# Output projection with three pairs of PSUM banks: logits transposes in the tile's own banks, work ranked by tile number

## The chip, the cores and the metric

The kernel runs on one core of one Trainium2 chip. The metric is the device time of one execution in microseconds (us), median of several runs. The engines are TensorE (PE, with its weight loads as PEld), VectorE (DVE), ScalarE (ACT), GpSimd (POOL) and SyncE (SP), which here only issues transfers. PSUM, the memory that TensorE writes, has eight banks; a tile of 128 rows by 512 columns of 32-bit numbers fills one.

## The reference, cut to what matters

Two layers of a transformer with a mixture of experts (MoE). The change touches what stands in each layer between attention and MoE:

```python
o = jnp.concatenate([o_a, o_b, o_c], axis=-1) @ w_out[l]      # (1024, 1024) @ (1024, 1024)
x = layer_norm(DEEPNORM_ALPHA * x + g1 * o, ln1_g[l], ln1_b[l])
h2 = modulate(x, sh2, sc2)                                    # a second layer norm, scale and shift
# ec_moe(h2, ...): router logits h2 @ w_router, softmax over 16 experts,
# each expert takes its top 128 tokens, gated FFN, scatter-add
x = layer_norm(DEEPNORM_ALPHA * x + g2 * ec_moe(h2, ...), ln2_g[l], ln2_b[l])
```

There are 1024 latent tokens (8 tiles of 128) in both layers; in layer 0 alone the 256 context tokens (2 tiles) go the same way with weights of their own modulation. No expert can start before all 1024 tokens have their routing scores, because top-k runs over tokens.

## The kernel before, in words

One function, `p4`, holds the stage; it runs once per layer. A tile `i` goes through these steps:

- Loads on SP's queue: `ot` (the attention output, transposed, L1684, for the first two tiles its last quarter apart, L1687), `rb` (softmax denominators, L1692, two transfers), `x` (the residual, L1698; two buffers).
- Preparation: `den` (L1705) multiplies by the denominators, `ohi` (L1715 on DVE, L1717 on ACT) and `olo` (L1720) split the 32-bit operand into two parts that TensorE multiplies at full rate. From the third tile on this is POOL and ACT.
- Projection on PE: 48 matmuls of 512 columns (L1737, L1738, L1739), in 8 groups of 6, into a pair of PSUM banks `po`, one bank for each half of the 1024 columns. There are two such pairs.
- Norms in place in the pair, on DVE: gate (L1745), add the residual (L1851), statistics (L1772 twice, L1778, L1779, and a power on POOL, L1782), normalize (L1795, L1798). ACT reads the pair once for the copy `ac` that the MoE accumulates into (L1860). Then a second norm: statistics again, L1795, and two halves of L1804 that write the result to SBUF as `t`.
- Routing: 8 transposes of `t` on PE (L1882) into the banks `tp` (two, one for each half), a copy of each half to SBUF `hT` on ACT (L1887, one buffer), 8 logits products (L1896), maximum (L1900), exponential (L1904), reciprocal (L1907), scaling (L1910), one transpose of the shares (L1919) and a copy into `aff` (L1923).

Context tiles differ: ACT copies the projection out of PSUM (L1750) and POOL and DVE do the norms in SBUF. After the eighth latent tile, 16 rounds of top-8 on DVE (L2008, L2009, L2011) pick the tokens; rounds 13 to 16 of layer 0 also serve the context tiles. Then the indices drive a gather, and the MoE begins.

The order of instructions on every engine is written by a planner, `Plan`. Each operation has an engine, a planned cost, a lag until others may use its result, a list of what it needs, and slots (how many buffers of a kind exist). The planner repeatedly takes the operation that can start earliest by its own clock; among those that can start at the same time it takes the largest sum of `way` (planned time from this operation to the end of everything that depends on it) and `rank`. The two lines that decide are:

```python
first = min(t for t, o in at) + self.SLACK
t, o = min(((t, o) for t, o in at if t <= first), key=lambda c: (-c[1]["way"] - c[1]["rank"], c[0], c[1]["n"]))
```

Most operations of tile `i` have the rank `old`, which is -3 times `i` before. The engines then execute that order, in order; where real times differ from planned ones an engine stands at its next instruction.

Of the kernel before, what the change touches and what calls it, by code (L numbers as in the profile page):

```python
# [8 lines left out]
F32 = mybir.dt.float32  # L9
# [4 lines left out]
AF = mybir.ActivationFunctionType  # L14
# [195 lines left out]
class Kern:  # L210
# [1368 lines left out]
    def p4(self, l):  # L1579
        nc, d = self.nc, self.d  # L1580
# [28 lines left out]
        if not last:  # L1609
            nc.gpsimd.memset(aff[64:80], -1.0)  # L1610
        ve, ac, po, pe, sy = "dve", "act", "pool", "pe", "sync"
        P = Plan(ported=True, ot=3, rb=3, x=2, oh=3, t1=4, po=2, tp=2, hT=1, lg=2, ac=1, raw=4, w=4)
        eng = {ve: nc.vector, po: nc.gpsimd}
        tt = {ve: 1.16, po: 2.32}
        load = lambda cost, f, **k: P.op(sy, cost, f, lag=2.2, **k)
# [51 lines left out]
        for i, (t, cond) in enumerate(tiles):  # L1667
            q = {}
# [6 lines left out]
            row0 = t * 128 - ctx * NL  # L1675
            src = self.s_o[part][:, :, cs].rearrange("c p q -> p c q")
            gain, scale, shift = range(3)
            old = -3.0 * i
            H = {k: P.new(k) for k in ("ot", "rb", "x", "oh", "t1", "hT", "ac")}

            def ld_o(q=q, src=src, i=i):
# [17 lines left out]
            a = load(1.2, ld_o, new=[H["ot"]], rank=old)  # L1699
            c = load(0.4, ld_c, use=[H["ot"]], after=[a], rank=old - 20.0) if i < 2 else a  # L1700
            b = load(1.2, ld_r, new=[H["rb"]], after=late[part], rank=old)
            x = load(1.46, ld_x, new=[H["x"]], rank=old)

            def den(q=q, i=i):
                (nc.vector if i < 2 else nc.gpsimd).tensor_tensor(q["ot"][:, 0:6], q["ot"][:, 0:6], q["rb"], op=ALU.mult)  # L1705
# [22 lines left out]
            for n in range(2):  # L1728
                o = None
                for k in range(4):  # L1730
                    def mm(q=q, n=n, k=k):
                        if n == 0 and k == 0:
                            q["o"] = self.rot(ps, [128, 2, 512], F32, "po", 2)
                        o, ns = q["o"][:, n], slice(n * 512, n * 512 + 512)
                        for j in (2 * k, 2 * k + 1):
                            wh, wl = whi[k][:, j % 2, ns], wlo[k][:, j % 2, ns]
                            nc.tensor.matmul(o, q["hi"][:, j], wh, start=j == 0, stop=False)  # L1737
                            nc.tensor.matmul(o, q["hi"][:, j], wl, start=False, stop=False)  # L1738
                            nc.tensor.matmul(o, q["lo"][:, j], wh, start=False, stop=j == 7)  # L1739
                    o = P.op(pe, 1.395, mm, [parts[k], W[k], o or first], new=[hp] if n == 0 and k == 0 else [],  # L1740
                             use=[H["oh"], hw[k]] + ([hp] if n or k else []), rank=old)
                    first = first or o

                def gate(q=q, n=n, cond=cond):
                    nc.vector.tensor_tensor(q["o"][:, n], q["o"][:, n], rows[cond][0][:, n * 512:n * 512 + 512], op=ALU.mult)  # L1745

                def out(q=q, n=n):
                    if n == 0:
                        q["t1"] = self.rot(p, [128, D], F32, "t1", 4)
                    nc.scalar.activation(q["t1"][:, n * 512:n * 512 + 512], q["o"][:, n], AF.Copy)  # L1750

                def gate_c(q=q, n=n, cond=cond):
                    ns = slice(n * 512, n * 512 + 512)
                    nc.gpsimd.tensor_tensor(q["t1"][:, ns], q["t1"][:, ns], rows[cond][0][:, ns], op=ALU.mult)
                if ctx:
                    o = P.op(ac, 0.6, out, [o, *gated[-1:]], new=[H["t1"]] if n == 0 else [],
                             use=[hp] + ([H["t1"]] if n else []), rank=old)
                    gated.append(P.op(po, 1.24, gate_c, [o, lrow[cond][0], *gated[-1:]], use=[H["t1"], hrow[cond][0]], rank=old))
                else:
                    gated.append(P.op(ve, 0.68, gate, [o, lrow[cond][0], *gated[-1:]], use=[hp, hrow[cond][0]], rank=old))  # L1760
# [29 lines left out]
            def affine_o(dep, g, b, uses, new=None, q=q):  # L1790
# [16 lines left out]
                if new is None:  # L1807
                    o = P.op(ve, 1.28, f2, [o], **u)
                    return [o, o]
                o1 = P.op(ve, 0.7, lambda: f3(0), [o], new=[new], **u)  # L1810
                return [o1, P.op(ve, 0.7, lambda: f3(1), [o1], use=u["use"] + [new], rank=old)]

            def affine(dep, kind, g, b, uses, q=q):

# [58 lines left out]
            P.op(sy, 1.46, put2, o, use=[H["t1"]], lag=2.2, rank=old)  # L1873
            c = []
            for h in range(2):
                ht = P.new("tp")

                def tr(q=q, h=h):
                    tp = q["tp", h] = self.rot(ps, [128, 4, 128], F32, "tp", 2)
                    for k in range(4):  # L1880
                        kk = h * 4 + k
                        nc.tensor.transpose(tp[:, k], q["t1"][:, kk * 128:kk * 128 + 128], self.ident)  # L1882

                def cp(q=q, h=h):
                    if h == 0:
                        q["hT"] = self.rot(p, [128, KC, 128], F32, "hT", 1)
                    nc.scalar.activation(q["hT"][:, h * 4:h * 4 + 4], q["tp", h], AF.Copy)  # L1887
                z = P.op(pe, self.CT if ctx else 0.44, tr, [o[h]], new=[ht], use=[H["t1"]], rank=old)
                c.append(P.op(ac, 0.49, cp, [z, *c[-1:]], new=[H["hT"]] if h == 0 else [],
                              use=[ht] + ([H["hT"]] if h else []), rank=old))  # L1890
            hl = P.new("lg")

            def logits(q=q):
# [17 lines left out]
            o = P.op(pe, self.CG if ctx else 1.75, logits, [*c, lw], new=[hl], use=[H["hT"]], rank=old)  # L1911
            o = P.op(ve, 0.1, top, [o], use=[hl], rank=old)
            o = P.op(ac, 0.3, ex, [o], use=[hl], rank=old)
            o = P.op(ac, 0.25, share, [P.op(ve, 0.15, rel, [o], rank=old)], rank=old)
            ha = P.new("lg")

            def turn(q=q):
# [72 lines left out]
    CT, CG = 0.44, 1.75  # L1990
    KINDS = "dd", "ff"
    TE = "pp"
    LP = 0
    ER = -100.0, -100.0
    WR, WS, HD, AB = (5.0, 10.0), (8.0, 4.0), (1, 1), (5.0, 5.0)

# [528 lines left out]
```

## Time and profile before

| | |
|---|---|
| median of 3 runs | 3002.39 us (2997.36 to 3002.39) |
| the profiled execution's own time | 2998.05 us |
| its span, first to last instruction | 2996.3 us |
| TensorE's mean granted clock | 0.936 of full |
| busy share of the span: PE, DVE, ACT, POOL | 88%, 73%, 53%, 30% |
| layer 0: first projection matmul to first top-k instruction | 601.6 to 780.4 us |
| layer 1: the same | 2148.4 to 2321.4 us |

The shares over the whole span are averages over stages with different limits; the two stretches in the last lines are where the change acts.

### The profile page before, as it was taken

The page shows a single profiled execution, that of the slowest core. Times are in us where ns is not written, and L with a number is a line of the kernel's source. Part 1 is how long each engine was busy: PE and PEld are TensorE (multiplying, and loading weights), DVE is VectorE, ACT ScalarE, POOL GpSimd, SP SyncE. Part 2 cuts the span into 40 slices and gives each one's busy share as a digit, 9 for nine tenths or more (in the row PEclk, how much of TensorE's full clock was granted, in tenths as well). Part 3 has the DMA queues.
Part 4 walks back from the last instruction along what each step waited for, and adds up shares of the span by engine and source line. Part 5 has one row for each costly group of instructions (what it writes and reads, how often), then busy time and mean ns, then how long its engine had stood idle before and what let it go on. Part 6 is the DMA issues. An engine that isn't in the chain of part 4 may idle for free.

```text
span 2996.3 us, 37302 instructions
## 1 busy us (share of the span) xinstructions
PE 2632.8 (88%) x13657; PEld 2066.0 (69%) x13657; DVE 2186.5 (73%) x3048; ACT 1588.1 (53%) x2023; POOL 886.2 (30%) x652
## 2 busy tenths in 40 slices
PE   7998888868569999999999499999867499999995
PEld 4986444446468888888888388655556377777774
DVE  6367597456769998888887835566556788888888
ACT  4224767612245656656666353686412367777774
POOL 2045787232312120201110416685120211111113
PEclk8999999978779999999999699999977699999998
DMA  6254734472268888888886414563452699999983
GB/s 241 79 177 145 207 127 121 121 222 102 89 238 317 319 313 312 311 312 313 313 310 229 159 64 150 174 188 94 137 168 106 261 360 374 375 374 367 367 348 133
DMA packets 204352, 682.85 MB, mean 228 GB/s; under 512 B 25637, under 2 KB 97630, under 8 KB 148870
## 3 DMA queue, kind: packets, MB, share of 16 engines
q1 hardware_dynamic: 191834, 641.23, 59.2%
q0 software_dynamic: 12336, 39.25, 5.2%
q8 instruction: 107, 1.75, 0.2%
q14 instruction: 75, 0.61, 0.1%
HBM read 600.45 MB, written 79.84 MB: 227 GB/s over the span
## 4 chain that ended last, share of the span: by engine, by line
PE 58%; DVE 7%; DMA 3%; issue 2%; ACT 1%; POOL 1%; SPq 0%; DVEq 0%; POOLq 0%; ACTq 0%
PE gu L2145 12%; PE gu L2146 6%; PE gu L2184 4%; PE gu L2185 4%; PE gu L2186 4%; PE O L1183 3%; PE gu L2226 2%; PE gu L2217 2%; PE gu L2240 2%; PE gu L2227 2%; PE gu L2228 2%; PE gu L2241 2%; PE gu L2239 2%; PE pj L736 1%; PE pj L737 1%
## 5 line engine op out<-in xcount | busy, mean ns | idle before, releaser
L2071 DVE TENSOR_TENSOR lo<-raw,hi 128x2048 fp32r<-128x2048 f32 x284 | 640.7, 2282 | 6.8 <-ACT hi L2065 6.8
L2065 ACT ACTIVATE hi<-raw 128x2048 fp32r<-128x2048 f32 x289 | 551.8, 1912 | 87.2 <-PE gu L2185 39.9
L2145 PE MATMUL gu<-xt,hi 128*128 128x320 f32 x2048 | 529.6, 333 | 0.9 <-DVE xt L2131 0.9
L2146 PE MATMUL gu<-xt,lo 128*128 128x192 f32 x2048 | 513.6, 251 | 0.0
L1257 POOL TENSOR_TENSOR cy<-cy,csq 128x512 f32<-128x512 f32 (+1 forms) x300 | 386.7, 1303 | 110.4 <-ACT csq L1253 101.1
L2261 POOL DMA_INDIRECT s_acc<-yo,i x31 | 76.3, 2463 | 1121.5 <-DVE yo L2259 1121.5
L2146 PEld LDWEIGHTS gu<-xt,lo 128*128 128x128 f32 x2048 | 393.0, 192 | 0.6
L2145 PEld LDWEIGHTS gu<-xt,hi 128*128 128x128 f32 x2048 | 386.2, 189 | 1.8 <-DVE xt L2131 1.1
L1183 PE MATMUL O<-P,v 128*65 128x512 f32 (+7 forms) x592 | 280.2, 562 | 11.9 <-ACT P L1176 11.6
L1253 ACT ACTIVATE csq<-ch,cw 128x512 f32<-128x512 f32 (+1 forms) x300 | 198.9, 673 | 47.0 <-POOL cy L1257 43.6
L2184 PE MATMUL gu<-hi,xt 128*128 128x512 f32 x512 | 204.3, 399 | 0.0
L2185 PE MATMUL gu<-hi,xt 128*128 128x512 f32 x512 | 202.8, 396 | 0.0
L2186 PE MATMUL gu<-lo,xt 128*128 128x512 f32 x512 | 202.6, 396 | 0.0
L735 PE MATMUL pj<-hhi,whi 128*128 128x512 f32 (+1 forms) x512 | 188.5, 368 | 9.4 <-ACT whi L249 9.4
L737 PE MATMUL pj<-hhi,wlo 128*128 128x512 f32 (+1 forms) x512 | 188.1, 367 | 1.5 <-DVE wlo L252 1.5
L736 PE MATMUL pj<-hlo,whi 128*128 128x512 f32 (+1 forms) x512 | 188.1, 367 | 0.0
L2071 DVE TENSOR_TENSOR lo<-more,hi 128x2048 fp32r<-128x2048 f32 x80 | 182.0, 2282 | 0.0
L2065 ACT ACTIVATE hi<-more 128x2048 fp32r<-128x2048 f32 x80 | 152.1, 1906 | 19.5 <-issue 10.0
L366 DVE CUSTOM_DVE_ANT_0 adj<-adw,srow,bmod 128x1024 bf16<-128x1024 f32 x96 | 133.8, 1394 | 34.4 <-DMA adw<-in_wmt 32.7
L1176 ACT ACTIVATE P<-ST 128x512 f32<-128x512 f32 (+1 forms) x200 | 114.6, 581 | 51.7 <-PE ST L1159 28.5
L1737 PE MATMUL po<-hi,ohi 128*128 128x512 f32 x288 | 122.8, 426 | 20.3 <-DVE ohi L1715 16.9
L1739 PE MATMUL po<-hi,olo 128*128 128x512 f32 x288 | 119.2, 414 | 3.4 <-DVE olo L1720 2.6
(319 smaller groups left out, 5787.4 us busy)
## 6 DMA issues: line engine op xcount, KB each, us to landing
raw<-in_wmoe SPq DMA_DIRECT2D x289, 1024.0 KB
more<-in_wmoe SPq DMA_DIRECT2D x80, 1024.0 KB
adw<-in_wmt SPq DMA_DIRECT2D x24, 1024.0 KB
srow<-in_wmoe SPq DMA_DIRECT2D x15, 1024.0 KB
wraw<-in_win SPq DMA_DIRECT2D x26, 512.0 KB
x<-in_x SPq DMA_DIRECT2D x16, 512.0 KB
adw<-in_wmt SPq DMA_DIRECT2D x16, 512.0 KB
q<-s_q SPq DMA_DIRECT2D x64, 128.0 KB
```

The source lines that it names most:

```text
L736: nc.tensor.matmul(o[:, :w], whi[:, k], hlo[:, k, sl], start=False, stop=False)
L737: nc.tensor.matmul(o[:, :w], wlo[:, k], hhi[:, k, sl], start=False, stop=k == 7)
L1183: nc.tensor.matmul(o[:V1, o0:o0 + w], self.v[:, t["kt"], t["v"] * V1:t["v"] * V1 + V1], t["P"][:, :w], start=t["first"], stop=t["last"] is ...
L1253: nc.scalar.activation(z[:, :w], h, AF.Copy, scale=c)
L1257: nc.gpsimd.tensor_tensor(st["y"], st["y"], st.pop(("z", t))[:, :w], op=ALU.add)
L2065: self.nc.scalar.activation(h, self.S["raw", i], AF.Copy)
L2071: eng.tensor_tensor(lo, r, h.bitcast(F32), op=ALU.subtract)
L2145: nc.tensor.matmul(o[:, f, :320], hi[:, k, fs], xt[:, k], start=k == 0, stop=False)
L2146: nc.tensor.matmul(o[:, f, :192], lo[:, k, fs], xt[:, k, :192], start=False, stop=k == 7)
L2184: nc.tensor.matmul(o, xt[:, kk, 0], hi[:, k], start=kk == 0, stop=False)
L2185: nc.tensor.matmul(o, xt[:, kk, 1], hi[:, k], start=False, stop=False)
L2186: nc.tensor.matmul(o, xt[:, kk, 0], lo[:, k], start=False, stop=kk == 7)
```

## The change

It does these things in `p4`, for both layers:

- The slots `tp` (two banks) are gone and `po` has three pairs instead of two; 2x2 + 2 + 2 banks become 3x2 + 2.
- The 8 transposes of a tile write into the tile's own pair, half by half, once the second norm has read that half; ACT copies from there. The pair is held until that copy.
- Ranks go down by 12 for each tile instead of 3 (`ORD`). The residual of the second tile is raised by 5 (`XE`).
- The two halves of the last norm step no longer depend on one another, have a planned cost of 0.72 instead of 0.7, the second half a rank lower by 0.5, and both a planned lag of 1.0 (all tiles but the last). The scaling of the shares gets a planned lag of 2.0 (all tiles but the last). Lags are numbers for the planner; they put no wait into the program.
- `LP`, used nowhere, is removed.

```diff
-        P = Plan(ported=True, ot=3, rb=3, x=2, oh=3, t1=4, po=2, tp=2, hT=1, lg=2, ac=1, raw=4, w=4)
+        P = Plan(ported=True, ot=3, rb=3, x=2, oh=3, t1=4, po=3, hT=1, lg=2, ac=1, raw=4, w=4)
...
-            old = -3.0 * i
+            old = -self.ORD[l] * i
...
-            x = load(1.46, ld_x, new=[H["x"]], rank=old)
+            x = load(1.46, ld_x, new=[H["x"]], rank=old + (self.XE if i == 1 else 0.0))
...
-                            q["o"] = self.rot(ps, [128, 2, 512], F32, "po", 2)
+                            q["o"] = self.rot(ps, [128, 2, 512], F32, "po", 3)
...
-                o1 = P.op(ve, 0.7, lambda: f3(0), [o], new=[new], **u)
-                return [o1, P.op(ve, 0.7, lambda: f3(1), [o1], use=u["use"] + [new], rank=old)]
+                wait = 1.0 if i < len(tiles) - 1 else None
+                o1 = P.op(ve, 0.72, lambda: f3(0), [o], new=[new], lag=wait, **u)
+                return [o1, P.op(ve, 0.72, lambda: f3(1), [o], use=u["use"] + [new], rank=old - 0.5, lag=wait)]
...
-                ht = P.new("tp")
-
                 def tr(q=q, h=h):
-                    tp = q["tp", h] = self.rot(ps, [128, 4, 128], F32, "tp", 2)
                     for k in range(4):
                         kk = h * 4 + k
-                        nc.tensor.transpose(tp[:, k], q["t1"][:, kk * 128:kk * 128 + 128], self.ident)
+                        nc.tensor.transpose(q["o"][:, h, k * 128:k * 128 + 128], q["t1"][:, kk * 128:kk * 128 + 128], self.ident)
...
-                    nc.scalar.activation(q["hT"][:, h * 4:h * 4 + 4], q["tp", h], AF.Copy)
-                z = P.op(pe, self.CT if ctx else 0.44, tr, [o[h]], new=[ht], use=[H["t1"]], rank=old)
+                    nc.scalar.activation(q["hT"][:, h * 4:h * 4 + 4], q["o"][:, h].rearrange("p (a b) -> p a b", a=4), AF.Copy)
+                z = P.op(pe, self.CT if ctx else 0.44, tr, [o[h]], use=[H["t1"], hp], rank=old)
                 c.append(P.op(ac, 0.49, cp, [z, *c[-1:]], new=[H["hT"]] if h == 0 else [],
-                              use=[ht] + ([H["hT"]] if h else []), rank=old))
+                              use=[hp] + ([H["hT"]] if h else []), rank=old))
...
-            o = P.op(ac, 0.25, share, [P.op(ve, 0.15, rel, [o], rank=old)], rank=old)
+            o = P.op(ac, 0.25, share, [P.op(ve, 0.15, rel, [o], rank=old)], rank=old,
+                     lag=2.0 if i < len(tiles) - 1 else None)
...
-    LP = 0
+    ORD = 12.0, 12.0
+    XE = 5.0
```

## Rows read from the trace of the kernel before

**Rows 1.** The page's second part: busy tenths of PE in 40 slices of 74.9 us each.

```profile
PE   7998888868569999999999499999867499999995
```

**Rows 2.** Busy time by stretch: from:to, length, then busy us and instruction count of PE, PEld, DVE, ACT and POOL, the granted clock, the share of the DMA engines, GB/s. The first two are the stage in each layer, the third a stretch without waits at full clock, then one two-tile run of matmuls, the first halt of PE in layer 0, and the top-k of layer 0.

```profile
601.60:780.40 178.80, 135.49 (x627) 109.16 (x628) 104.36 (x170) 35.70 (x71) 43.15 (x33) 0.84 0.50 153
2148.40:2321.40 173.00, 129.82 (x584) 105.13 (x584) 105.11 (x170) 31.85 (x68) 35.12 (x28) 0.81 0.49 157
613.00:621.00 8.00, 8.00 (x36) 6.41 (x36) 3.26 (x2) 0.00 (x0) 0.00 (x0) 1.00 1.06 361
...
2271.50:2296.10 24.60, 24.48 (x100) 19.44 (x99) 9.77 (x15) 2.13 (x5) 0.54 (x1) 0.93 0.11 43
629.00:653.80 24.80, 1.11 (x5) 0.71 (x4) 15.75 (x26) 3.88 (x5) 14.31 (x10) 0.59 0.81 202
780.40:845.00 64.60, 22.48 (x108) 17.98 (x106) 57.00 (x122) 18.48 (x25) 28.61 (x17) 0.66 0.40 159
```

**Rows 3.** Waits of PE in the stage: who waited, for whom, us in total, times, the longest. The first line is layer 0, the other two layer 1.

```profile
PE tp L1882 <- DVE t L1804: 25.6, 2, 22.9
...
PE lg L1919 <- ACT e L1910: 21.7, 4, 9.1
PE tp L1882 <- DVE t L1804: 15.5, 1, 15.5
```

**Rows 4.** Groups by line in layer 1's stage (8 tiles): what one tile costs DVE. Instructions, busy us, mean ns, then idle time before them and who ended it.

```profile
L1772 DVE BATCH_NORM_STATS2 p4st<-po 128x6 f32<-128x512 f32 x32 | 21.7, 692 | 7.5 <-PE po L1739 5.3 <-ACT ac L1860 1.6
...
L1804 DVE SCALAR_TENSOR_TENSOR t<-po,p4nr,raw 128x512 f32<-128x512 f32 x16 | 11.6, 743 | 0.4 <-POOL p4nr L1782 0.3
...
L1745 DVE TENSOR_TENSOR po<-po,raw 128x512 f32<-128x512 f32 x16 | 11.2, 699 | 45.2 <-PE po L1739 44.9
L1851 DVE SCALAR_TENSOR_TENSOR po<-x,po 128x512 f32<-128x512 f32 x16 | 11.1, 696 | 0.6
L1798 DVE SCALAR_TENSOR_TENSOR po<-po,p4nr,lnb 128x1024 f32<-128x1024 f32 x8 | 10.3, 1285 | 0.3
L1795 DVE SCALAR_TENSOR_TENSOR po<-po,mv,raw 128x1024 f32<-128x1024 f32 x8 | 10.3, 1284 | 1.9 <-ACT ac L1860 1.9
L1795 DVE SCALAR_TENSOR_TENSOR po<-po,mv,lng 128x1024 f32<-128x1024 f32 x8 | 10.2, 1278 | 0.0
...
L1778 DVE BATCH_NORM_AGGREGATE mv<-p4st 128x2 f32<-128x12 f32 x16 | 3.2, 202 | 0.2
...
L1779 DVE TENSOR_SCALAR p4nr<-mv 128x1 f32<-128x1 f32 x16 | 2.5, 154 | 0.6
...
L1900 DVE TENSOR_REDUCE sm<-lg 128x1 f32<-128x16 f32 x8 | 1.3, 166 | 6.4 <-PE lg L1896 6.4
L1907 DVE RECIPROCAL sm<-sm 128x1 f32<-128x1 f32 x8 | 1.3, 157 | 1.5 <-ACT e L1904 1.5
```

**Rows 5.** The same view, layer 1, the other engines' steps of a tile.

```profile
L1887 ACT ACTIVATE hT<-tp 128x512 f32<-128x512 f32 x16 | 9.2, 595 | 10.0 <-PE tp L1882 5.5 <-PE lg L1896 4.4
L1782 POOL TENSOR_TENSOR p4nr<-p4nr,mhalf 128x1 f32<-128x1 f32 x16 | 8.7, 546 | 62.0 <-DVE p4nr L1779 61.9
...
L1860 ACT ACTIVATE ac<-po 128x1024 f32<-128x1024 f32 x8 | 8.2, 1024 | 58.7 <-DVE po L1798 49.4 <-DMA s_acc<-ac 9.3
```

**Rows 6.** Timeline of PE, single stretches: start, length, instruction, [idle before, releaser]. Two projection matmuls at full clock that are 30 matmuls apart, four transposes, the logits products of one tile (two instructions for each of 8), and the transposes of shares that end two halts, one period apart. The line at 623.14 is where the late quarter of `ot` arrived.

```profile
613.06 0.39 PE L1737 MATMUL po<-hi,ohi 128*128 128x512 f32 x1
...
620.06 0.39 PE L1737 MATMUL po<-hi,ohi 128*128 128x512 f32 x1
...
623.14 0.50 PE L1737 MATMUL po<-hi,ohi 128*128 128x512 f32 x1 [1.52 <-DVE ohi L1715]
...
680.38 0.63 PE L1882 MATMUL tp<-ident,t 128*128 128x128 f32 x4
681.28 1.96 PE L1896 MATMUL lg<-wr,hT 128*128 128x16 f32 x16 [0.27 <-ACT hT L1887]
...
2232.27 0.38 PE L1919 MATMUL lg<-ident,e 128*16 128x128 f32 x1 [9.08 <-ACT e L1910]
...
2269.65 0.38 PE L1919 MATMUL lg<-ident,e 128*16 128x128 f32 x1 [5.66 <-ACT e L1910]
```

**Rows 7.** Timelines of DVE and POOL around the first tiles of layer 0 (626 to 647) and of layer 1 (2170 to 2182): the first gate in each layer, the second tile in PSUM waiting for its residual, statistics waiting for ACT's reading of the pair, POOL at the first tile's power, and in layer 1 the gate that follows the last of the first 96 matmuls.

```profile
626.24 0.70 DVE L1745 TENSOR_TENSOR po<-po,raw 128x512 f32<-128x512 f32 x1 [2.21 <-PE po L1739]
...
639.69 0.69 DVE L1851 SCALAR_TENSOR_TENSOR po<-x,po 128x512 f32<-128x512 f32 x1 [7.32 <-DMA x<-in_x]
...
646.98 0.70 DVE L1772 BATCH_NORM_STATS2 p4st<-po 128x6 f32<-128x512 f32 x1 [1.09 <-ACT ac L1860]
...
638.03 0.57 POOL L1782 TENSOR_TENSOR p4nr<-p4nr,mhalf 128x1 f32<-128x1 f32 x1
...
2170.16 0.70 DVE L1745 TENSOR_TENSOR po<-po,raw 128x512 f32<-128x512 f32 x1 [4.09 <-PE po L1739]
...
2177.13 0.70 DVE L1745 TENSOR_TENSOR po<-po,raw 128x512 f32<-128x512 f32 x1 [2.18 <-PE po L1739]
...
2181.74 0.58 POOL L1782 TENSOR_TENSOR p4nr<-p4nr,mhalf 128x1 f32<-128x1 f32 x1
```

**Rows 8.** Timeline of DVE at the top-k: layer 0's first instruction, and its wait for the context tiles.

```profile
780.38 0.69 DVE L2008 MAX8 tv<-aff 48x8 f32<-48x512 f32 x1 [5.67 <-ACT aff L1923]
...
832.32 0.69 DVE L2008 MAX8 tv<-aff 80x8 f32<-80x512 f32 x1 [2.46 <-ACT aff L1923]
```

## The prediction

> **What bounds the kernel now.** I read the page's busy tenths first [rows 1]. Most slices have PE at 8 or 9; in the tenths 4 to 7 about slices 9 to 12 and 29 to 32 the reader sees the stages between attention and MoE, where PE stands. The change acts in two of them, so next comes busy time by stretch [rows 2]. From the first projection matmul to the first top-k instruction layer 0 takes 178.8 us with PE busy for 135.5, layer 1 takes 173.0 with 129.8: some 43 us a layer without PE. DVE is busy for 104 and 105. So no engine is full: a chain is. Whose chain, the waits of PE say [rows 3]. Layer 0 loses 25.6 us to transposes that wait for the last norm step, 22.9 of them at once, and layer 1 15.5 at once and 21.7 in four waits for the shares. PE projects two tiles, finds no free pair, and stands until DVE has carried the first of the two through both norms. The same shows from DVE's side: the gate waits 44.9 us in all for the projection [rows 4]. The engines take turns.
>
> Does the time of this stage come through to the end? Top-k needs every token, the experts need top-k, and top-k starts behind the last latent tile's copy into `aff` [rows 8]. I count a microsecond here as one of the total.
>
> **Third pair: the steady pace.** PE's work for a tile: 48 matmuls at 7.00/30 = 0.233 us [rows 6] are 11.2; 8 transposes are two groups of 0.6, logits products 1.9, the shares' transpose 0.3 [rows 6]. Sum 14.6 us. DVE's: the eleven groups add up to 94.7 us for 8 tiles, 11.8 each [rows 4]. If one tile is finished before the next is begun, DVE also stands while ACT reads the pair for `ac`: 1.09 us in the row [rows 7], so 13.0 with handovers. A pair is held for 14.6 us of PE's time and then for DVE's chain, transposes and copies, about 13 + 3: 31 us, and three pairs allow a tile each 10. So PE sets 14.6 us a tile, if it never waits. Before, two tiles take 37.4 (the halts that end at 2232.3 and 2269.7 mark the period [rows 6]), 18.7 each: 24.6 of matmuls [rows 2], then the rest of DVE's chain uncovered. I take 15.5, since DVE is at 13.0 of 14.6 and each engine runs in a fixed order.
>
> Here the page "PSUM — Partial Sum Buffer" of the Trainium skill (PSUM bank collisions raise a hardware error) speaks against the change: no two engines may touch one bank at once, two reads included. The row with 1.09 us agrees. By that rule transposes and copies also serialize inside the tile's own banks, which the old separate banks spared; since PE writes a half while ACT copies the other, the sum is the same, and if each copy of 0.6 us held up PE twice a tile it would be 1.2 us a tile more.
>
> **Third pair: the start.** Layer 0's first two tiles leave PE at 629.0, where its first halt begins [rows 2]. A third tile follows at once, its inputs having been prepared before: 11.2 us, to 640.2. The residual of the third tile can only be fetched when the first has been added (two buffers); it ended DVE's wait at 639.69 [rows 7], in time. The fourth tile needs the first pair. POOL delivered the first tile's power at 638.03 + 0.57, behind splits of later tiles [rows 7]. If that stays: 638.6, L1798 1.3, ACT's reading 1.0 with one statistics under it, the other 0.7, mean and sum 0.36, L1795 1.3, L1804 1.5 [rows 4, 5], transposes 1.2, copies 1.2 and handovers: 648. If tile rank brings the power forward nothing is lost: 640.2. I take 645. In layer 1 the same walk from 2177.1, where the first 96 matmuls end [rows 7], gives 2188.3 for the third tile, and from the power at 2181.74 [rows 7] 2191 for the fourth. I take 2191.
>
> **The tail.** After the eighth tile's last matmul: gate, addition, statistics 2.1, mean and sum 0.35, L1795 and L1798 2.6, `ac` and one statistics 1.7, mean and sum 0.35, L1795 1.3, L1804 1.4 [rows 4, 5], transposes and copy 1.2, logits 1.9, softmax 1.1, transpose and copy 0.6. That is 14.6 us, and with some twenty handovers of 0.1 us 16.5. The powers on POOL (0.55) pass beside L1795.
>
> **The sum.** From the fourth tile's start: five tiles' matmuls 56.0, the other PE work of seven tiles 7 x 3.4 = 23.8, allowance 5 x 0.9 = 4.5, tail 16.5: 100.8 us. Layer 0: 645 + 100.8 = 745.8, against 780.4: 34.6 saved. Layer 1: 2191 + 100.8 = 2291.8, against 2321.4: 29.6. Together 64 us. The profiled execution took 2998.05; the median shown is 4.3 above it. So 2934 becomes 2938.
>
> **The rest of the diff.** Rank 12 is what makes DVE finish a tile before it begins another: by the planned costs the way from a tile's last matmul to its transposes is 12.0 (gate, addition, two statistics, mean, power, two normalizations, two statistics, mean, power, normalization, last step with lag 1.0), so a gate one tile later ranks about even with the older tile's last steps and below its other ones. A matmul has 13.5 to 24 more way than its tile's transposes: those of the next tile still go before the older tile's transposes, those two tiles on mostly behind. That order is the forecast. The lags only leave room in it; price nothing, covered by the matmuls between. The first tiles' late quarter of `ot` (rank 20 lower) now passes the third tile's loads on SP's queue; between nothing and the 1.5 us that PE waited for it [rows 6]; I take nothing. `XE` moves one 0.5 MB load by a place or two: nothing, for the second tile's residual was there first. Context tiles hold their pairs until their copies; nobody comes after them. Their chain must keep up with a top-k that starts earlier: top-k waited 2.46 us for it once [rows 8]. PE is free of latent matmuls sooner, so between 0 and 5 us more saved; I take nothing. The split last step saves no work.
>
> **Rivals.**
> - *DVE becomes the bound.* Finishing tile by tile leaves it nothing to do while ACT reads (1.09), POOL raises to the power (0.55 twice, with handovers 1.4) and PE ends a half. 11.8 + 1.1 + 1.4 + 1.5 is 16 us a tile. From the first gates, 626 and 2170 [rows 7], 8 x 16 + 7 for routing gives 761 and 2305: 19 and 16 saved, 2998 - 35 + 4 = 2967. For it: the row of 1.09 and POOL's late power. Against: powers run under L1795, and next tiles' gates fill holes. Chance 0.22.
> - *One layer alone gains.* Layer 0's loads (0.81 of the DMA engines in the first halt [rows 2]) keep the fourth tile back, or the context chain sets top-k's end as the 2.46 hints: 3002 - 30 = 2972, chance 0.05.
> - *Nothing changes.* A load paces the stage, as the residual did for 7.32 us [rows 7]. But DMA falls to 0.11 in the later tiles [rows 2]. 3002, chance 0.05.
> - *Slower.* Place: PE's queue. The planner sets a tile's transposes between matmuls two tiles on; if DVE is later than planned, PE stands there with ready matmuls behind it, as it stood 9.08 us for shares [rows 6]. Price: the delay, at 14 places (7 a layer). It decides from 64/14 = 4.6 us a place; with 9 at each, 2938 + 126 = 3064. Against: the chain after the last matmul measures 9.8 to the end of L1804 without handovers, under the planned 12.0. Chance 0.08.
>
> **How the numbers follow.** Forecast 0.60, and the four rivals as given. Its own range: no stall at either start (4.8 + 2.7), pace 14.6 (9), context waits gone (5) give 2917; pace 16.5 in both layers (10) and 1.2 us for the banks over 16 tiles (19) give 2967. For 8 in 10 the range is 2915 to 2985: it takes in the two rivals that gain less and leaves no change and slower out, 0.13, with some of the edges. The three runs differ by 0.17%, so 0.2%, 6 us, is about what can be told apart. Faster 0.86, same 0.06, slower 0.08.
>
> **What would show it.** PE's waits on L1804 of 22.9 and 15.5 us fall to under 8 each, those on the shares (21.7) vanish from the middle of the stage. Its matmuls run in series longer than 96, and the granted clock of the two stretches rises above 0.84 and 0.81. DVE's gates wait some 15 us for the projection instead of 45. The first top-k instruction comes near 746, and 143 us after layer 1's first matmul (173 before). If DVE is busy 95% of the stage, the first rival holds; if transposes wait over 4 us at most tiles, the last. MoE stretches should keep their lengths; if they don't, the prediction is wrong there, not here.

## The result, and the profile after

Measured in turn on one chip, the changed kernel took 2927.44 us and the kernel before 2999.88 (medians of four runs each); the ratio is 0.9769, 95% interval 0.9738 to 0.98. Measured once more, beside two of the experiments below, it gave 2928.69 against 2996.05, ratio 0.9779 (0.9765 to 0.9792). The profiled execution took 2927.74 us; its span, 2926.0, is 70.3 less than before. One of the five executions of an experiment below (own banks and third pair) took 6457.73 us, and no profile shown is of it.

First PE's busy tenths by fortieths of the span, from the page of the changed kernel:

```profile
PE   7998888979489999999999499999996699999995
```

A slice is 73 us. Of the hollow that [rows 1] has in each layer, slice 11 is left in layer 0, the top-k behind the stage, and slices 31 and 32 in layer 1, the tail and top-k. Busy time by stretch, in the columns of [rows 2]; first the two stages (first projection matmul to first top-k instruction), then the pipelined part of each stage, and the tail of layer 1:

```profile
603.20:749.20 146.00, 138.36 (x665) 113.00 (x666) 105.01 (x175) 38.22 (x74) 49.27 (x37) 0.95 0.63 192
2112.60:2251.60 139.00, 121.21 (x584) 98.56 (x584) 105.74 (x170) 32.63 (x68) 34.05 (x28) 0.91 0.58 194
...
650.20:740.00 89.80, 88.15 (x450) 72.26 (x450) 72.42 (x124) 27.14 (x56) 24.49 (x23) 0.98 0.42 145
2157.00:2230.00 73.00, 71.54 (x367) 58.82 (x366) 61.34 (x102) 18.64 (x42) 17.30 (x18) 0.98 0.39 146
2230.00:2251.50 21.50, 9.13 (x51) 7.73 (x50) 11.94 (x21) 5.29 (x13) 1.08 (x2) 0.61 0.47 176
```

The stages went from 178.8 and 173.0 us [rows 2] to 146.0 and 138.9. Layer 1 has the same work in it, 584 instructions on PE in both, and DVE's busy time is 105 us as before; layer 0's stage has 665 on PE instead of 627, since more of the context tiles' matmuls now fall before the top-k. In the middle of either stage PE is busy for 98% at a granted clock of 0.98. The waits of PE in the two stages (for whom, us in total, times, the longest), layer 0 first:

```profile
PE po L1880 <- DVE t L1804: 4.7, 3, 3.6
PE lg L1894 <- ACT hT L1885: 0.7, 1, 0.7
...
PE po L1880 <- DVE t L1804: 9.4, 3, 7.6
...
PE lg L1918 <- ACT e L1908: 3.1, 2, 1.8
```

The 25.6 and 15.5 us on the last norm step [rows 3] are 4.7 and 9.4, and 7.6 of the 9.4 are the tail, where nothing else is left to do; the 21.7 on the shares are 3.1. DVE's gates in layer 1 wait 3.0 us for the projection, where they waited 44.9 [rows 4] and the prediction named some 15. The 70.3 us by place: layer 0's first matmul comes 1.6 us later, its stage is 32.8 shorter, the way from the first top-k instruction to the first transposes of the MoE (L2129) 3.3 shorter; layer 1's first matmul comes 35.8 earlier, so between the layers another 1.2 are gone, layer 1's stage is 34.1 shorter, and 0.4 falls behind it.

### The profile page after: what moved, and what is told of

Read it like the earlier page. It is cut to its first block, busy times and chain, and to the rows that moved or that the text cites. A ratio compares the mean times of both kernels' runs of the same rounds, so it can differ in the third digit from the quotient of the medians.

```text
span 2926.0 us, 37297 instructions
## 1 busy us (share of the span) xinstructions
PE 2619.4 (90%) x13657; PEld 2057.6 (70%) x13657; DVE 2184.7 (75%) x3048; ACT 1587.8 (54%) x2023; POOL 884.3 (30%) x652
## 5 line engine op out<-in xcount | busy, mean ns | idle before, releaser
L1737 PE MATMUL po<-hi,ohi 128*128 128x512 f32 x288 | 121.7, 423 | 21.4 <-DVE ohi L1715 18.9
L2153 ACT ACTIVATE t<-gu 128x320 f32<-128x320 f32 x128 | 55.5, 433 | 119.3 <-PE gu L2146 119.1
```

## The experiments

The change has three parts that can be had one by one: the rank of a tile (3 or 12), the place of the transposes (banks of their own kind, called separate here, or the tile's own), and the number of pairs. Three pairs with separate banks don't fit, so there are six combinations; the lags and `XE` come on top. All kernels with own banks also have the last norm step in two independent halves, as the change has; what that split does by itself was not tried. **Theory A**, the prediction's: PE stood because it found no free pair, and the third pair ends that. **Theory B**: the rank does it, because two tiles that DVE carries side by side come free together, whatever their number.

Medians in us, with the ratio to the kernel before as it was measured beside each:

| | rank 3 | rank 12 |
|---|---|---|
| two pairs, separate banks | 2998.59 (before) | with `XE` 2932.51, 0.9782 (0.9757 to 0.9806); with lags and `XE` 2933.03, 0.9793 (0.9777 to 0.9808) |
| two pairs, own banks | 2982.91, 0.9947 (0.9928 to 0.9967) | 2964.6, 0.9892 (0.9877 to 0.9907), with lags and `XE` |
| three pairs, own banks | 2963.25, 0.9879 (0.9861 to 0.9898) | 2928.69, 0.9779 (0.9765 to 0.9792), the change; without lags and `XE` 2935.52, 0.9791 (0.9774 to 0.9809) |

And the stages, from the first row of L1737 to the first of the top-k in each trace, with the period of a tile in the middle of layer 0, from the starts of its transposes (with rank 3 from the starts of blocks of matmuls):

| kernel | layer 0, us | layer 1, us | us a tile |
|---|---|---|---|
| before | 178.8 | 173.0 | 17.9 |
| rank alone (with `XE`) | 146.9 | 145.7 | 14.1 |
| rank alone with lags and `XE` | 155.3 | 142.3 | 14.0 |
| own banks alone | 171.1 | 173.1 | 16.2 |
| own banks and third pair | 166.0 | 156.0 | in blocks |
| the change with two pairs | 164.2 | 160.0 | 16.2 |
| the change | 146.0 | 138.9 | 13.0 |
| the change, second profile | 147.7 | 138.8 | 13.7 |
| the change without lags | 146.3 | 151.5 | 14.1 |
| less matmul work | 149.7 | 140.1 | 13.8 |
| less DVE work | 149.0 | 145.4 | 13.2 |
| `ac` in halves | 146.4 | 141.9 | 13.0 |
| rank 30 | 148.3 | 152.0 | 13.3 |

The two profiles of the change differ by 1.8 us in layer 0 and by 0.7 us a tile, so less than that tells nothing. The profile of the rank alone with lags and `XE` is of an execution of 2943.67 us, 10.6 above its median; in its layer 0 one wait for `ohi` at the start takes 7.8 us, where the rank alone has 2.6.

**Rank alone** (with `XE`), in the kernel before:

```
-            old = -3.0 * i
+            old = -12.0 * i
-            x = load(1.46, ld_x, new=[H["x"]], rank=old)
+            x = load(1.46, ld_x, new=[H["x"]], rank=old + (5.0 if i == 1 else 0.0))
```

> The kernel before (two pairs, separate banks for the transposes) with rank 12 a tile alone. Theory A (the pairs do it): with two pairs PE can project one tile while DVE carries the other; a pair is then held for 11.2 us of matmuls and a chain of 11 to 12 us, so a tile each 12 at the least but in strict turns with the other PE work, 16 to 18.7 us a tile: stages of 160 to 178 us, total 2965 to 3000 us. Theory B (the rank does it, the third pair adds little): stages within 4 us of 146.0 and 138.9, total 2927 to 2940 us.

It took 2932.51 us: 66 of the change's 67 to 72, with two pairs and the separate banks. Theory A falls. Its PE row in the middle of layer 0 (busy time by stretch), and then DVE in order of time (start, us, line, what; in brackets the wait before):

```profile
655.00:740.00 85.00, 84.62 (x445) 69.99 (x444) 69.35 (x115) 26.43 (x52) 23.04 (x20) 1.00 0.39 135
...
669.31 0.70 DVE L1745 TENSOR_TENSOR po<-po,raw 128x512 f32<-128x512 f32 x1 [0.46 <-PE po L1739]
...
674.10 1.28 DVE L1795 SCALAR_TENSOR_TENSOR po<-po,mv,lng 128x1024 f32<-128x1024 f32 x1
...
675.50 1.29 DVE L1798 SCALAR_TENSOR_TENSOR po<-po,p4nr,lnb 128x1024 f32<-128x1024 f32 x1
...
679.67 1.28 DVE L1795 SCALAR_TENSOR_TENSOR po<-po,mv,raw 128x1024 f32<-128x1024 f32 x1
681.06 1.41 DVE L1804 SCALAR_TENSOR_TENSOR t<-po,p4nr,raw 128x512 f32<-128x512 f32 x2
683.28 0.70 DVE L1745 TENSOR_TENSOR po<-po,raw 128x512 f32<-128x512 f32 x1 [0.81 <-PE po L1739]
```

One tile's first norm, second norm and last step stand in a row, and then comes the next tile's gate: 13.2 us from its own gate to the end of its last step. PE is busy for 84.62 of 85 us at clock 1.00: two pairs saturate it. In the kernel before DVE does this, in the same view:

```profile
666.80 0.70 DVE L1745 TENSOR_TENSOR po<-po,raw 128x512 f32<-128x512 f32 x1 [7.77 <-PE po L1739]
...
682.71 1.28 DVE L1795 SCALAR_TENSOR_TENSOR po<-po,mv,raw 128x1024 f32<-128x1024 f32 x1
683.90 1.28 DVE L1795 SCALAR_TENSOR_TENSOR po<-po,mv,lng 128x1024 f32<-128x1024 f32 x1
685.09 0.74 DVE L1804 SCALAR_TENSOR_TENSOR t<-po,p4nr,raw 128x512 f32<-128x512 f32 x1
685.75 1.28 DVE L1798 SCALAR_TENSOR_TENSOR po<-po,p4nr,lnb 128x1024 f32<-128x1024 f32 x1
686.94 0.74 DVE L1804 SCALAR_TENSOR_TENSOR t<-po,p4nr,raw 128x512 f32<-128x512 f32 x1
...
692.41 1.41 DVE L1804 SCALAR_TENSOR_TENSOR t<-po,p4nr,raw 128x512 f32<-128x512 f32 x2
```

Two tiles alternate instruction by instruction, the older one's second norm (`raw`) with the younger one's first (`lng`, `lnb`). The older one takes 20.9 us from gate to last step (666.8 to 687.7). Both pairs stay occupied meanwhile, and then both come free, at 687.7 and 693.8, within the 11.2 us of one tile's matmuls.

**Own banks alone** (two pairs, rank 3, no lags, no `XE`): the changed kernel with

```
-        P = Plan(... t1=4, po=3, hT=1, ...)
+        P = Plan(... t1=4, po=2, hT=1, ...)
-                            q["o"] = self.rot(ps, [128, 2, 512], F32, "po", 3)
+                            q["o"] = self.rot(ps, [128, 2, 512], F32, "po", 2)
-    ORD = 12.0, 12.0
-    XE = 5.0
+    ORD = 3.0, 3.0
+    XE = 0.0
...
-                wait = 1.0 if i < len(tiles) - 1 else None
+                wait = None
...
-                     lag=2.0 if i < len(tiles) - 1 else None)
+                     lag=None)
```

> Two pairs, transposes in the tile's own banks, old rank, no lags and no XE: the banks' cost alone. The pair is held longer by the second norm, transposes and copies, some 8 us a tile, and two tiles go together, so the halts of PE grow by about 8 us for each pair of tiles: with three halts that are followed by more matmuls in a layer, 20 to 24 us a layer later, total 3035 to 3050 us. If instead the shared bank costs nothing because the pair was free only at the end of both norms anyhow, the total stays at 2995 to 3005 us.

Both expectations were wrong: it gained 16 us. PE in order of time in layer 0:

```profile
650.97 1.09 PE L1880 MATMUL po<-ident,t 128*128 128x128 f32 x4 [23.30 <-DVE t L1804]
...
669.91 1.07 PE L1880 MATMUL po<-ident,t 128*128 128x128 f32 x8
672.20 0.60 PE L1737 MATMUL po<-hi,ohi 128*128 128x512 f32 x1 [1.23 <-ACT hT L1885]
```

The first halt stays (23.3 us, as the 22.9 of [rows 3]). But a pair now comes free only with the copy of its own transposes, and those follow each other on PE, so the pairs come free one after the other and the blocks of 96 matmuls break into blocks of 48: 16.2 us a tile instead of 17.9, although PE waits 0.7 to 1.2 us for ACT's copy seven times. The longer hold was priced, the regular order that it enforces was not. How much of the 16 us the split of the last norm step has in it is open.

**Own banks and third pair** (rank 3, no lags, no `XE`): as above with `po=3` and `"po", 3`.

> The third pair and the tiles' own banks, with rank 3 a tile as before, and without the lags and XE. Theory A (the pairs do it: PE stood because it found no free pair): PE goes on over the third tile as in the changed kernel, stages of 145 to 152 us in layer 0 and 138 to 145 in layer 1 against 146.0 and 138.9, total 2927 to 2942 us. Theory B (the rank does it: with rank 3 DVE still carries two tiles through the norms side by side, so that pairs come free together): PE runs three tiles and then stands for 10 us or more, some 16 to 17 us a tile, stages near 160 and 153, total 2955 to 2970 us.

It took 2963.25 us, half of the gain; own banks alone had 16 of these 35 us. The profile is from a second run, 2960.97 us:

> The third pair and the own banks with rank 3, once more, for an undisturbed profile (the one of the first run was taken with every matmul at twice its time). By the time of the first run, 2963.25 us median, about half of the gain is there. Theory B (the rank decides): the order of PE's queue still has two or three tiles' matmuls in one block and then a halt on the last norm step; stages of about 160 and 158 us. Theory A (the pairs decide and something small is missing): matmuls and transposes alternate tile by tile, with short waits, and what is lost sits in the tail.

```profile
639.40 0.40 PE L1739 MATMUL po<-hi,olo 128*128 128x512 f32 x1
653.72 1.09 PE L1880 MATMUL po<-ident,t 128*128 128x128 f32 x4 [13.93 <-DVE mv L1778]
656.28 1.12 PE L1880 MATMUL po<-ident,t 128*128 128x128 f32 x4 [1.47 <-DVE t L1804]
658.97 0.80 PE L1737 MATMUL po<-hi,ohi 128*128 128x512 f32 x1 [1.57 <-ACT hT L1885]
```

Three tiles' matmuls in one block, and then the halt: 19.2 us from 639.8 to 659.0 with 2.2 of transposes in it, where [rows 2] has 24.8 behind two tiles. The third pair puts the halt off by a tile; it doesn't end it. Theory B, in time and in order.

**The change with two pairs** (`po=2` and `"po", 2` alone), and **the change without own banks and third pair** (the kernel before with rank, lags and `XE`), beside **the change itself**:

> The changed kernel with two pairs instead of three, all else as in the change: transposes in the tile's own banks, rank 12, lags, XE. A pair is then held for the 11.2 us of matmuls, DVE's chain of 11 to 12 and the transposes and copies, 2 to 3: some 25 us, and two pairs give one tile each 12.5 at best; PE has to do logits and shares of older tiles in the gaps. If the third pair is what lets the rank work with the own banks: 15 to 16 us a tile instead of 14, 8 to 16 us a layer, total 2943 to 2960 us. If two pairs are enough here too: total 2925 to 2937 us.

> The kernel before with rank 12, the lags and XE: all of the change without the third pair and without the own banks. The rank alone gave 2932.51 us median. If what is left to the changed kernel, about 5 us, is owed to the lags (which cost the rank alone 7.6 us of waiting in layer 1's fourth tile): total within 4 us of the changed kernel's, 2924 to 2932 us. If it is owed to the third pair (PE projects the third tile while DVE has the first, and is never idle from 632.9 to 639.7 us): total 2930 to 2936 us, with a first halt of PE of about 7 us in each layer.

> The changed kernel itself, for a comparison beside the two others on the same chip: 2927 us, 2922 to 2932, ratio to before 0.975 to 0.978. Both theories expect the same of it; which of the two kernels with two pairs is within 0.2% of it tells whether the third pair gives anything.

2964.6, 2933.03 and 2928.69 us: the first is 4.6 us above the first of its two ranges, the second in the second of its ranges (PE's first halts are 8.1 and 4.3 us), the third as expected. With rank 12 the own banks cost 32 us, and the third pair gives back 36. Together they are worth 4.3 us, 0.15%, and the two intervals (0.9777 to 0.9808, 0.9765 to 0.9792) overlap: not to be told from nothing. Why own banks need the third pair shows in PE's order with two pairs, first its waits from 655 to 740 us, then the rows:

```profile
PE lg L1894 <- ACT hT L1885: 3.4, 5, 0.7
...
675.90 1.04 PE L1880 MATMUL po<-ident,t 128*128 128x128 f32 x8
677.62 1.96 PE L1894 MATMUL lg<-wr,hT 128*128 128x16 f32 x16 [0.69 <-ACT hT L1885]
```

Between the transposes and the logits, while ACT copies, PE has no matmul whose pair is free: one pair is with DVE, the other holds the transposes. It waits 0.69 us, and in most places its granted clock falls as well (last section): 16.2 us a tile. From 655 to 740 us PE has no other wait and is busy for 81.57 of 85 us, so it is these places that cost the 2 us a tile. With the separate banks or with a third pair six matmuls stand in that place.

**The change without lags and `XE`**:

> The changed kernel without the planned lags of the last norm step and of the shares and without XE. The prediction priced them at nothing: total within 6 us of 2927 (2921 to 2933), waits of PE before transposes and shares within 4 us of those of the changed kernel (11 and 4 us in the two layers together without the tail). Rival: the lags are what keeps matmuls in front of transposes that DVE is late for; without them PE waits 1 to 2 us at each of the 14 transposes and 14 shares, 20 to 40 us, total 2947 to 2967 us.

2935.52 us, 2.5 above the expected range, and the intervals overlap with those of the change. Layer 0's transposes wait 8.3 us in all instead of 4.7, and layer 1's 17.2 instead of 9.4. Layer 1's stage is 151.5 us in its profile, 12.6 longer than in both profiles of the change. The prediction's nothing was some 7 us too low by the medians and 4 by the ratios; whether the total differs by more than scatter stays open, and the lags and `XE` were not tried apart.

**Which engine paces the changed kernel.** Two cuts, one on each engine.

```
-                            nc.tensor.matmul(o, q["hi"][:, j], wl, start=False, stop=False)
-                            nc.tensor.matmul(o, q["lo"][:, j], wh, start=False, stop=j == 7)
+                            nc.tensor.matmul(o, q["hi"][:, j], wl, start=False, stop=j == 7)
```

> The changed kernel without the product of low inputs and high weights (16 of the 48 matmuls of a tile left out): 3.7 us of PE's work less a tile. From 655 to 740 us the changed kernel has PE busy for 83.35 of 85 us and DVE for 67.72. If PE is the bound: the pace falls from 13.9 us of PE's work to DVE's 13.0 at most, the first three tiles end 11 us earlier: each stage 12 to 25 us shorter (sum of the two stages 235 to 261 us instead of 285), and PE now halts on the last norm step for over 1 us at most tiles. If DVE is the bound: only the first tile comes 3.7 us earlier, sum 275 to 280 us.

```
-                    gated.append(P.op(ve, 0.68, gate, [o, lrow[cond][0], *gated[-1:]], ...))
+                    gated.append(o)
```

> The changed kernel without the gate's multiplication of the latent tiles (left out): 1.4 us of DVE's work less a tile. If PE is the bound: only the start and the tail, where DVE's chain stands alone, are shorter, 1 to 3 us a layer, sum of the two stages 279 to 284 us. If DVE is the bound: 8 x 1.4 = 11 us a layer, sum 260 to 265 us.

They took 2925.17 and 2932.6 us (one run each), against 2925 to 2934 of the change itself: neither cut gains. None of the four expectations came: the stages sum to 289.7 and 294.4 us, against 284.9 and 286.5 in the two profiles of the change. Busy time from 655 to 740 us of the cut on PE, with DVE's waits there and PE's in layer 0's stage, and then of the cut on DVE:

```profile
655.00:740.00 85.00, 69.77 (x330) 56.42 (x329) 66.55 (x112) 24.52 (x50) 20.99 (x21) 0.86 0.37 131
...
DVE p4st L1771 <- ACT ac L1860: 6.5, 6, 1.1
DVE sm L1897 <- PE lg L1893: 5.3, 3, 2.4
...
PE po L1879 <- DVE t L1803: 19.8, 6, 8.7
```

```profile
655.00:740.00 85.00, 82.53 (x429) 67.77 (x429) 61.94 (x103) 25.45 (x51) 22.73 (x20) 0.99 0.40 140
```

Without a third of its matmuls PE halts in front of the transposes (19.8 us in layer 0's stage, 24.2 in layer 1's), its clock falls to 0.86, and a tile takes 13.8 us. I read that as DVE's turn: 11.8 of work [rows 4], and in these 85 us 6.5 of waits for `ac`, 5.3 for PE's logits and 3.0 for powers. Without the gate DVE is idle for 23 of the 85 us and PE is at 97%: 13.2 us a tile. So the two turns lie within one microsecond of each other, and no cut on one engine shows. For DVE this is argued, not shown, since in the cut on PE each engine also waits for the other. Why the two kernels' stages are longer than those of the change was not traced.

**A cut on DVE's wait**: `ac` in two halves, the second half of the pair first.

```
+                y1 = P.op(ac, 0.6, lambda f=grown_half: f(1), o, new=[H["ac"]], use=[hold], rank=old)
+                y = P.op(ac, 0.6, lambda f=grown_half: f(0), [y1], use=[hold, H["ac"]], rank=old)
+                o = [o[0], y1]
```

> ACT's copy ac is made in two halves, the second half of the pair first, so that DVE's statistics and ACT never read the same half: DVE's wait of 1.1 us a tile goes. If PE is the bound the wait is covered in the middle and what is won is in the tail, 1 us a layer, and in the fourth tile's start: total 2923 to 2930 us beside 2928. If DVE is the bound: 8 us a layer, total 2910 to 2915 us. It could cost instead: two instructions of ACT, 0.7 us each in place of one of 1.0, in front of exp and share, 0 to 5 us more.

2924.97 us, 0.9766 (0.9749 to 0.9783). DVE's wait for `ac` in layer 0's stage falls from 7.6 us to 4.0, the longest from 1.1 to 0.7, and the stages are no shorter (146.4 and 141.9): as for a wait that PE covers. 0.13% under the change by the ratios, with overlapping intervals, is no gain that could be told.

**Rank 30**:

> Rank 30 a tile instead of 12, three pairs as in the change: all of an older tile's work goes before any of a younger one. If it matters only that DVE finishes a tile before the next (the step of the prediction): the same, total 2924 to 2934 us. If matmuls of the next two tiles have to go before the older tile's transposes, as at 12, so that PE is covered while DVE works: with 30 PE's transposes, logits and shares stand at their planned times with short waits and lower clock, 1 to 2 us at each of 14 tiles, total 2942 to 2957 us.

2937.84 us, 0.9806 (0.9789 to 0.9824), between the two expectations, some 9 us above the change by the medians; the intervals just overlap. Layer 1's stage is 13 us longer than in both profiles of the change. The middle isn't slower (13.3 us a tile). The start is another: the first tile's transposes come 29.7 us after the first matmul instead of 41.0, and then the second tile's wait:

```profile
654.61 1.94 PE L1880 MATMUL po<-ident,t 128*128 128x128 f32 x8 [5.20 <-DVE t L1804]
```

In layer 1 the same place costs 5.6 us, and DVE's last step waits 8.8 us for powers on POOL. So more counts than that DVE finishes a tile before the next; how much of the loss each of these is was not separated.

## Why the prediction was right, and where it was not

**The time** was right (2938 forecast, 2927 measured), and so was the mechanism that it saw in the result: DVE finishes a tile's norms before it begins those of the next (only the next one's gates and additions go in between), matmuls fill PE meanwhile, the stages are 30 to 35 us shorter, and the MoE stretches keep their lengths.

**The step that failed is the one that names the cause.** "PE projects two tiles, finds no free pair, and stands", so the third pair was credited with the steady pace. The observation is right and the inference is not: no pair was free because DVE carried two tiles at once. The prediction knew that rank 12 lines DVE up, and made that a condition of its pace; it did not ask what is left for a third pair once it holds. Rank 12 with two pairs gives 66 us; own banks and third pair under rank 3 put the halt off by a tile and end at half the gain. The prediction's own numbers would have shown it: it holds a pair for 14.6 us on PE and some 16 behind that, 31 with the own banks, which is 15.5 a tile for two pairs (16.2 measured). Without transposes and copies in the pair, 3 us less, it is 14, PE's own pace (14.1 measured). That division was made for three pairs and not for two. That it comes so near to 16.2 is partly luck: that kernel's tiles take 15.0 us where the clock holds and 16.4 to 16.5 where it falls, and the sum knows nothing of the clock.

**The own banks** were priced at nothing. In this change that holds, as a sum of two large terms, -36 and +32. The rule of the page "PSUM — Partial Sum Buffer" of the Trainium skill (PSUM bank collisions raise a hardware error), which the prediction set against the change, speaks of one bank; a tile's halves lie in two, before and after, so it doesn't set the two kernels apart. The traces do. The prediction let PE write one half while ACT copies the other. In the changed kernel's trace none of the 36 copies has a transpose starting inside it; with the rank alone 10 of 36 have, as here in layer 1's tail (PE, then ACT):

```profile
2247.94 1.94 PE L1882 MATMUL tp<-ident,t 128*128 128x128 f32 x8 [5.71 <-DVE t L1804]
...
2249.06 0.60 ACT L1887 ACTIVATE hT<-tp 128x512 f32<-128x512 f32 x1 [4.47 <-PE tp L1882]
```

With three pairs that costs little: PE's waits for copies in the changed stages are 0.7 us in layer 0 and 2.4 in layer 1, so of the prediction's two sums the first, without the 1.2 us a tile, is the nearer. What it missed is that the pair's longer hold takes from PE the matmuls between transposes and logits as soon as there are only two.

**The sizes**, in the times of the profile before (the changed kernel's, less 1.6 us in layer 0 and plus 35.8 in layer 1, so that the first projection matmuls coincide):

| term | forecast | measured |
|---|---|---|
| layer 0, third tile's matmuls end | 640.2 | 638.9 |
| layer 0, fourth tile starts | 645 (bound 648) | 648.6 |
| layer 0, first top-k | 745.8 | 747.6 |
| layer 1, third tile ends, fourth starts | 2188.3, 2191 | 2189.3, 2192.2 |
| layer 1, first top-k | 2291.8 | 2287.3 |
| tail after layer 1's last matmul | 16.5 | 21.5 |
| way from first top-k to MoE in layer 0, shorter by | 0 (0 to 5) | 3.3 |
| saved in all | 64 | 70.3 |

Part of the nearness is luck, since errors of opposite sign cancel: in layer 1 the start is 1.2 us later than forecast, the five tiles behind it 10.7 shorter, the tail 5.0 longer.

The fourth tile in layer 0, in the changed kernel's own times: PE in order of time, POOL, and DVE:

```profile
644.15 1.94 PE L1880 MATMUL po<-ident,t 128*128 128x128 f32 x8 [3.64 <-DVE t L1804]
646.77 3.59 PE L1894 MATMUL lg<-wr,hT 128*128 128x16 f32 x16 [0.69 <-ACT hT L1885]
650.21 0.77 PE L1737 MATMUL po<-hi,ohi 128*128 128x512 f32 x1
...
640.23 1.80 POOL L1705 TENSOR_TENSOR ot<-ot,rb 128x768 f32<-128x768 f32 x1 [4.67 <-DVE po L1795]
642.00 0.56 POOL L1782 TENSOR_TENSOR p4nr<-p4nr,mhalf 128x1 f32<-128x1 f32 x1
...
642.59 1.41 DVE L1804 SCALAR_TENSOR_TENSOR t<-po,p4nr,raw 128x512 f32<-128x512 f32 x2 [2.50 <-POOL p4nr L1782]
```

The start came as late as the prediction's late case, but by other steps. The first tile's first power, which that case had late, is early now (632.0). Its second power stands behind a product of a later tile on POOL, DVE's last step waits 2.50 us for it, and PE has nothing that may go. Even so the pair is copied by 647.2, 645.6 in the times of the profile before. But PE does the first tile's logits before the fourth tile, which the sum had behind its start, and at a granted clock of 0.50 (644.1 to 650.2) they hold it up for 3.44 us, where 1.9 was entered.

**The pace.** PE's work is 14.1 us a tile where it is saturated (rank alone), against 14.6 in the sum, which added up busy times that overlap by 0.15 to 0.24 us at every change of group. The allowance of 0.9 a tile wasn't needed: waits of PE from 655 to 740 us are 1.6 us together. The 13.0 a tile of the change (13.7 in its second profile) is a little under PE's work, because matmuls are in hand when the series starts and are used up (252 go by for six tiles' transposes, 5.25 tiles' worth). From the fourth tile's start to the last matmul in layer 1 it is 73.6 us where the sum has 84.3. Of the 10.7, 6.8 is other work of two tiles that lies elsewhere (the first tile's transposes and logits before the fourth tile, the seventh's behind the last matmul), the rest is most of the allowance.

**The tail** is 5.0 us longer. The changed kernel's PE and DVE there, in order of time:

```profile
2229.87 0.66 PE L1880 MATMUL po<-ident,t 128*128 128x128 f32 x4
2231.22 0.66 PE L1880 MATMUL po<-ident,t 128*128 128x128 f32 x4 [0.69 <-ACT hT L1885]
...
2243.48 1.09 PE L1880 MATMUL po<-ident,t 128*128 128x128 f32 x4 [7.62 <-DVE t L1804]
2245.25 1.11 PE L1880 MATMUL po<-ident,t 128*128 128x128 f32 x4 [0.69 <-ACT hT L1885]
2246.16 3.43 PE L1894 MATMUL lg<-wr,hT 128*128 128x16 f32 x16
...
2228.41 1.41 DVE L1804 SCALAR_TENSOR_TENSOR t<-po,p4nr,raw 128x512 f32<-128x512 f32 x2
2230.05 0.70 DVE L1745 TENSOR_TENSOR po<-po,raw 128x512 f32<-128x512 f32 x1 [0.23 <-PE po L1739]
...
2241.93 1.41 DVE L1804 SCALAR_TENSOR_TENSOR t<-po,p4nr,raw 128x512 f32<-128x512 f32 x2
2249.63 0.17 DVE L1898 TENSOR_REDUCE sm<-lg 128x1 f32<-128x16 f32 x1 [6.29 <-PE lg L1894]
```

L1804 ends at 2243.3, 13.3 us after the last matmul, where the sum has 9.8 and its handovers. The sum puts the gate, addition and statistics of one half behind it, and the trace those of both, three instructions of 0.7 us more: DVE is on the seventh tile until 2229.8, and then the eighth's first gate waits 0.23 us and is released by the last of the tile's 48 matmuls. In the profile before it is so too (1.03 us at the same place). The way from there is 8.2 us instead of the 4.8 and handovers of the sum: the halves' transposes go one after the other and the logits start 2.7 us after the first where 1.2 was entered (1.8 with the rank alone), and at the lower clock (0.61 granted in this stretch) they take 3.43 instead of 1.9.

**The rivals.** *DVE becomes the bound* at 16 us a tile did not come, but its place was nearer than its chance of 0.22 says: DVE's turn is 13 to 14 us, beside PE's 14. Its price was too high because the waits that it added one by one (`ac` 1.1, powers 1.4, halves 1.5) are partly filled with the next tile's gate and addition: from 655 to 740 us, six tiles, 6.5 us of waits for `ac` remain, 4.2 for powers and 0.8 for the projection. *PE's queue waiting at 14 places* decides from 4.6 us each; between the first tile and the tail the waits are 0.2 to 0.5. *One layer alone* and *nothing* are refuted by the two stages.

## What to carry to other kernels

When an engine stands for lack of a buffer, look first at how long each buffer is held and whether its consumer works on two at a time: ranking the consumer's work by tile gave here with two buffers what the third was thought to give. Price a merged buffer by its hold divided by the number of buffers, with the number before the change too, and try the parts of a change in all combinations, since two large terms of opposite sign (+32 and -36 us here) look like nothing in the sum. When two engines' turns are as near to each other as they seem to be here, a cut on one alone need not show.

## What the runs showed of the hardware

In the change with two pairs PE waits 0.69 us between transposes and logits, and behind most of these waits the granted clock falls. First the stretch from one such wait on, then two whole tiles, in the columns of [rows 2]:

```profile
661.10:666.90 5.80, 5.76 (x26) 4.92 (x27) 5.58 (x10) 1.15 (x4) 2.36 (x2) 0.71 0.43 129
675.90:692.40 16.50, 15.81 (x75) 12.81 (x74) 11.55 (x19) 4.11 (x9) 5.24 (x4) 0.90 0.36 127
692.40:707.40 15.00, 14.31 (x75) 11.75 (x74) 11.56 (x19) 4.03 (x9) 3.43 (x3) 1.00 0.24 95
```

In the first PE is busy for 5.76 of 5.80 us, and eight of the matmuls start 0.43 us apart instead of 0.23, the lower of the two levels (1.2 and 2.4 GHz): the eighteen matmuls up to the next share take 5.8 us where 18 x 0.233 are 4.2. Before it PE had done eight small transposes, the wait, and sixteen small logits products. It is not so at every such place: of the five waits from 655 to 740 us four have such a stretch behind them, and behind the one at 694.1 the eighteen matmuls take 4.3. So the wait alone does not decide it, and what does was not found. Where six matmuls stand between transposes and logits, in the kernel with the rank alone, the clock is 1.00 from 655 to 740 us.

The transposes of a tile's second half waited 0.69 us for ACT's copy of the first half in the tail (two places above), although the halves lie in different banks. Transposes into another tile's pair do run beside a copy (own banks and third pair: copy at 675.04, the other tile's transposes until 675.8). So the wait goes with the pair, not with a bank; whether the hardware needs it or only the program's semaphores make it was not tried.
